# The x loads of experts 0 to 3 as three transfers instead of two, in a batched-expert MLP

## The chip, the cores and the metric

The kernel runs on one core of one Trainium2 chip. The metric is the time of one execution on the device in microseconds (us). Lower is better. The core's engines are named as in the profile: PE (TensorE: matmuls and transposes; PEld is its weight load), DVE (VectorE), ACT (ScalarE), POOL (GpSimd) and SP (SyncE, which here only waits and issues transfers). Transfers run on 16 DMA engines that all issuing engines share.

## What is computed

Eight experts, each with its own input and its own two weight matrices:

```python
n_experts, capacity, hidden, expert_hidden = 8, 256, 512, 2048
# x (8, 256, 512), w1 (8, 512, 2048), w2 (8, 2048, 512), all float32
h = np.matmul(x, w1)
h = np.maximum(h, 0)
return np.matmul(h, w2).astype(np.float32)
```

In float32, one expert's w1 is 4.19 MB, its w2 the same, its x 0.52 MB. The kernel computes in bfloat16 and stores float32.

## The kernel before, in words

Sizes: E = 8 experts, C = 256 rows, H = 512, F = 2048; P = 128 partitions, MT = C / P = 2 row tiles, KT1 = H / P = 4, KT2 = F / P = 16, G = E / 2 = 4.

**Loading x.** x of experts 0 to 3 goes into `x_f` as float32, by transfers that SP issues in `load_x` (line 92). The view `x_r` puts two neighbouring rows of x on one partition, so for each expert a partition gets one piece of 2 x 512 x 4 B = 4 KB; a transfer of one expert is 128 such pieces, of two experts 256. x of experts 4 to 7 goes into `x_c`, cast to bfloat16 on the way, in one transfer that POOL issues (line 139).

**The frame.** Only the x loads of line 92 stand inside the Tile frame. `tc.close()` (line 97) ends it; in the trace the barrier that goes with it is booked under line 98: every engine waits there for every other. All else is issued behind it, with semaphores set by hand.

**POOL's queue behind the barrier.** POOL issues, in this order: x_c (line 139), w1 of experts 0 and 1 (line 129, `load_w1`), builds the identity matrix (lines 142 to 144), w2 of experts 0 and 1 (line 134, `load_w2`). All weights are cast to bfloat16 on the way. There are two buffers for w1 and two for w2, so each further w1 waits until ACT has done the first layer of the expert that holds the buffer, each further w2 until that expert's output is copied. The w2 of the last two experts comes in two parts (lines 136 and 137). The last transfer on POOL's queue is the output of experts 0 to 3 (line 163). SP issues the outputs of experts 4 to 6 (line 123) and 7 (line 125).

**Transposing x.** Four rounds, r = 0 to 3, take two experts each: a = 2r + b, where DVE does b = 0 and ACT does b = 1 (`take_x`). In a round, DVE and ACT each wait for x, cast or copy it into `x_b[:, b]` (line 174, in `cast`) and raise `t_xb`. PE waits until `t_xb` has both (`take(t_xb, 2)`, line 247 on; line 87 is the wait), transposes 8 tiles for each b into `pt[b]` (line 251), and DVE and ACT copy the result to `xe` (line 190 for experts 0 to 3, line 193 for 4 to 7). In rounds 0 and 1 the wait is for `s_x[r]`, the transfer that holds both experts of the round; from round 2 on for x_c.

**The two layers.** PE runs all four rounds of transposes first, then for each pair of experts the first layer of both (line 267, out of `pt_h`, with ReLU by DVE at line 216 and ACT at line 214) and the second layer of both (line 287, into `pt_o`, copied out at line 223). Ahead of each expert's layer PE waits on `t_w`, which SP raises when the weights have landed and, for the first layer, when x is transposed (SP's chain of waits, lines 105 to 125).

Of the kernel before, what the change touches and what calls it, by code (L numbers as in the profile page):

```python
# [9 lines left out]
def kernel(  # L10
# [20 lines left out]
    G = E // 2  # L31
# [28 lines left out]
    pt = [nc.alloc_psum_tensor(f"pt_tr{b}", [P, KT1 * MT, P], bf) for b in range(2)]  # L60

    sem = nc.alloc_semaphore
    s_x = [sem(f"s_x{i}") for i in range(G // 2)]
    s_xc = sem("s_xc")
    s_out = [sem(f"s_out{i}") for i in range(3)]
    s_w1 = [sem(f"s_w1_{e}") for e in range(E)]
# [24 lines left out]
    def load_x(e, n, i):  # L91
        ins = sp.dma_start(x_f[:, e:e + n], x_r[:, e:e + n]).then_inc(s_x[i], 16)
        return ins.ins.name

    for r in range(G // 2):
        tc.no_tile_sem_insts.add(load_x(2 * r, 2, r))
    tc.close()
    tc.compile()  # L98

# [69 lines left out]
    def cast(eng, r, b):  # L169

        a = 2 * r + b
        src = x_f[:, a] if a < G else x_c[:, MT * (a - G):MT * (a - G + 1)]
        copy = act.copy if eng is act else dve.tensor_copy
        copy(  # L174
            x_b[:, b].rearrange("p (t m) q -> p t m q", m=MT),
            src.rearrange("p m (q t) -> p t m q", t=KT1),
        ).then_inc(t_xb, 1)

    def take_x(eng, b):
        copy = act.copy if eng is act else dve.tensor_copy  # L180
        for r in range(G):
            if r < G // 2:
                eng.wait_ge(s_x[r], 16)
            elif r == G // 2:
                eng.wait_ge(s_xc, 16)
            cast(eng, r, b)
            eng.wait_ge(s_tr, 2 * r + b + 1)
            a, n = 2 * r + b, KT1 * C
            if a < G:
                copy(xe[:, a * n:(a + 1) * n], pt[b][:].rearrange("p j q -> p (j q)")).then_inc(s_xe[b], 1)  # L190
            else:
                xl = xe[:, G * n:].rearrange("p (l j q f) -> p l j q f", l=G, j=KT1 * MT, f=G)
                copy(  # L193
                    xl[:, :, :, :, a - G].rearrange("p l j q -> p j l q"),
                    pt[b][:].rearrange("p j (l q) -> p j l q", l=G),
                ).then_inc(s_xe[b], 1)
# [28 lines left out]

    act.sem_inc(t_ha, 1)
    take_x(act, 1)
    layers(act, 1, s_ha, s_oa, t_ha, s_act)

    dve.sem_inc(t_hb, 1)  # L230
    take_x(dve, 0)
    layers(dve, 0, s_hb, s_ob, t_hb, s_dve)

# [95 lines left out]
```

## Time and profile before

| what | value |
|---|---|
| time, median of 3 runs | 179.58 us (179.54 to 179.58) |
| the profiled execution | 179.67 us |
| its span, first to last instruction | 178.4 us |
| mean granted TensorE clock | 0.963 |
| transfers issued in all | 24, of which 2 load `x_f` |

The profile is that of one execution. "us to landing" of a transfer counts from its issue to the last of its 16 completions. Times within the trace are us from the span's start. A transfer's issue is an instruction of the issuing engine's queue (SPq, POOL) and lasts well under a microsecond; the bytes move later, on the DMA engines. GB/s are those written to the destination: a transfer that casts float32 to bfloat16 reads twice what it writes.

### The profile page before, as it was taken

What the parts mean: (1) busy time and instruction counts of PE and PEld (TensorE: products, weight loads), DVE (VectorE), ACT (ScalarE), POOL (GpSimd) and SP (SyncE); (2) the same over time, 40 slices, a digit from 0 to 9 for tenths busy, and PEclk for the clock granted to TensorE, in tenths of its full rate; (3) what the DMA queues carried; (4) which work ended last, traced back from release to release, by engine and by line L of the source; (5) the groups of instructions that cost most, each with busy time, mean ns of one, the idle gap of its engine ahead of it and who ended that gap; (6) DMA issues with size and microseconds to landing.
All of it is one profiled execution on the core that took longest, in us unless ns stands there. A gap on an engine that the chain in (4) does not pass through costs nothing. (4 is left out here: it accounts for less than half of the span.)

```text
span 178.4 us, 2360 instructions
## 1 busy us (share of the span) xinstructions
PE 131.5 (74%) x832; PEld 89.3 (50%) x832; DVE 37.3 (21%) x48; ACT 37.9 (21%) x49; POOL 12.4 (7%) x26
## 2 busy tenths in 40 slices
PE   0214479899949696899769695979495695998950
PEld 0213368796413295794224485954142694953410
DVE  0232653332010133131100231320101141311010
ACT  2455554222010122121100132220101122311010
POOL 3500000101010101001000101010202100000000
PEclk9999999999987999699969999999999999999996
DMA  5999989989989989989999998998998999999998
GB/s 181 349 234 235 228 184 235 235 176 235 235 176 235 235 184 228 235 191 220 235 206 206 235 220 191 235 232 180 235 235 176 235 235 192 201 214 225 280 417 353
DMA packets 4352, 40.90 MB, mean 229 GB/s; under 512 B 384, under 2 KB 384, under 8 KB 2176
## 3 DMA queue, kind: packets, MB, share of 16 engines
q0 software_dynamic: 3264, 36.70, 94.2%
q1 hardware_dynamic: 1088, 4.19, 6.1%
HBM read 71.30 MB, written 4.19 MB: 423 GB/s over the span
## 5 line engine op out<-in xcount | busy, mean ns | idle before, releaser
L267 PE MATMUL pt_h<-xe,w_sb 128*128 x512 | 65.0, 284 | 12.9 <-PEq L87 12.9
L267 PEld LDWEIGHTS pt_h<-xe,w_sb 128*128 x512 | 57.5, 147 | 21.0 <-issue 19.2
L287 PE MATMUL pt_o<-w_sb,ht_sb 128*128 x256 | 59.7, 393 | 9.7 <-PEq L87 9.7
L287 PEld LDWEIGHTS pt_o<-w_sb,ht_sb 128*128 x256 | 25.3, 100 | 42.7 <-issue 16.2
L216 DVE TENSOR_SCALAR ht_sb<-pt_h 128x512 bf16<-128x512 f32 x32 | 22.1, 692 | 51.7 <-PE pt_h L267 51.6
L214 ACT ACTIVATE ht_sb<-pt_h 128x512 bf16<-128x512 f32 x32 | 19.1, 597 | 56.7 <-PE pt_h L267 56.7
L251 PE MATMUL pt_tr<-identity,x_b 128*128 128x128 bf16 x64 | 7.5, 309 | 17.7 <-PEq L87 17.7
L223 DVE COPY out_sb<-pt_o 128x512 f32 x8 | 5.5, 692 | 66.1 <-PE pt_o L287 66.1
L223 ACT COPY out_sb<-pt_o 128x512 f32 x8 | 4.7, 586 | 64.3 <-PE pt_o L287 64.3
L251 PEld LDWEIGHTS pt_tr<-identity,x_b 128*128 128x128 bf16 x64 | 6.5, 143 | 18.4 <-issue 18.4
L129 POOL DMA_DIRECT2D w_sb<-in_w_dram x8 | 4.3, 534 | 71.3 <-ACTq L218 71.3
L134 POOL DMA_DIRECT2D w_sb<-in_w_dram x6 | 3.9, 652 | 35.3 <-ACT out_sb L223 35.2
L193 DVE COPY xe<-pt_tr 128x1024 bf16<-128x1024 bf16 x2 | 4.9, 2466 | 5.2 <-PE pt_tr L251 5.2
L193 ACT COPY xe<-pt_tr 128x1024 bf16<-128x1024 bf16 x2 | 4.9, 2465 | 4.1 <-PE pt_tr L251 4.1
L174 ACT CAST x_b<-x_f 128x1024 bf16<-128x1024 f32 x2 | 4.0, 2000 | 2.9 <-DMA x_f<-in_x_dram 2.9
L174 DVE CAST x_b<-x_f 128x1024 bf16<-128x1024 f32 x2 | 2.2, 1076 | 7.9 <-DMA x_f<-in_x_dram 7.9
L190 ACT COPY xe<-pt_tr 128x1024 bf16<-128x1024 bf16 x2 | 2.0, 1012 | 4.1 <-PE pt_tr L251 4.1
L190 DVE COPY xe<-pt_tr 128x1024 bf16<-128x1024 bf16 x2 | 1.4, 692 | 4.2 <-PE pt_tr L251 4.2
L136 POOL DMA_DIRECT2D w_sb<-in_w_dram x2 | 1.1, 531 | 17.0 <-ACT out_sb L223 17.0
L174 ACT COPY x_b<-x_c 128x1024 bf16<-128x1024 bf16 x2 | 2.2, 1118 | 0.0
L174 ACT ACT_TABLE_LOAD x1 | 1.3, 1283 | 2.6 <-PEq L98 2.6
L174 DVE COPY x_b<-x_c 128x1024 bf16<-128x1024 bf16 x2 | 1.4, 700 | 0.0
(9 smaller groups left out, 3.4 us busy)
## 6 DMA issues: line engine op xcount, KB each, us to landing
w_sb<-in_w_dram POOLq DMA_DIRECT2D x14, 2048.0 KB, 29.5
w_sb<-in_w_dram POOLq DMA_DIRECT2D x2, 1152.0 KB, 26.7
x_f<-in_x_dram SPq DMA_DIRECT2D x2, 1024.0 KB, 7.7
out_dram<-out_sb POOLq DMA_DIRECT2D x1, 2048.0 KB, 36.0
w_sb<-in_w_dram POOLq DMA_DIRECT2D x2, 896.0 KB, 30.4
out_dram<-out_sb SPq DMA_DIRECT2D x1, 1536.0 KB, 8.6
x_c<-in_x_dram POOLq DMA_DIRECT2D x1, 1024.0 KB, 9.9
out_dram<-out_sb SPq DMA_DIRECT2D x1, 512.0 KB, 5.8
```

What stands on the lines that cost most here:

```text
L129: pool.dma_start(w1_k[:, e % 2 * KT1:(e % 2 + 1) * KT1], w1_r[e]).then_inc(s_w1[e], 16)
L134: pool.dma_start(w2_k[:, k:k + KT2], w2_r[e]).then_inc(s_w2[e], 16)
L136: pool.dma_start(w2_k[:, k:k + CUT], w2_r[e, :, :CUT]).then_inc(s_w2[e], 16)
L174: copy(x_b[:, b].rearrange("p (t m) q -> p t m q", m=MT), src.rearrange("p m (q t) -> p t m q", t=KT1),).then_inc(t_xb, 1)
L190: copy(xe[:, a * n:(a + 1) * n], pt[b][:].rearrange("p j q -> p (j q)")).then_inc(s_xe[b], 1)
L193: copy(xl[:, :, :, :, a - G].rearrange("p l j q -> p j l q"), pt[b][:].rearrange("p j (l q) -> p j l q", l=G),).then_inc(s_xe[b], 1)
L214: act.activation(dst, ph[half][:], relu).then_inc(t_h, 1)
L216: dve.tensor_relu(dst, ph[half][:]).then_inc(t_h, 1)
L223: copy(outs[b], po[:, half]).then_inc(s_copied, 1)
L251: ins = pe.transpose(pt[b][:, j], x_b[:, b, j], identity[:])
L267: ins = pe.matmul(ph[i // 2][:, i % 2, :], ws[i % 2 * KT1 + kt], xs[kt], start=(kt == 0), stop=(kt == KT1 - 1),)
L287: ins = pe.matmul(po[:, m], hs[(kt - k0) * MT + m], ws[kt - k0], start=(kt == 0), stop=(kt == KT2 - 1),)
```

## The change

x of experts 0 and 1 comes in one transfer each (128 pieces of 4 KB), x of experts 2 and 3 together in a third (256 pieces). All three are issued by SP inside the frame, ahead of the barrier. There are three semaphores. In round 0 DVE waits for the first transfer and ACT for the second; in round 1 both wait for the third.

```diff
-    s_x = [sem(f"s_x{i}") for i in range(G // 2)]
+    s_x = [sem(f"s_x{i}") for i in range(3)]
...
-    for r in range(G // 2):
-        tc.no_tile_sem_insts.add(load_x(2 * r, 2, r))
+    for i, (e, n) in enumerate(((0, 1), (1, 1), (2, 2))):
+        tc.no_tile_sem_insts.add(load_x(e, n, i))
     tc.close()
     tc.compile()
...
         for r in range(G):
             if r < G // 2:
-                eng.wait_ge(s_x[r], 16)
+                eng.wait_ge(s_x[b if r == 0 else 2], 16)
             elif r == G // 2:
                 eng.wait_ge(s_xc, 16)
             cast(eng, r, b)
```

## The prediction

> **What bounds the kernel now.** I read the DMA parts of the page first, because the program moves far more bytes than it computes.
>
> ```profile
> q0 software_dynamic: 3264, 36.70, 94.2%
> HBM read 71.30 MB, written 4.19 MB: 423 GB/s over the span
> PE pt_o L287 4%; ACT out_sb L223 0%
> PE 131.5 (74%) x832; PEld 89.3 (50%) x832; DVE 37.3 (21%) x48; ACT 37.9 (21%) x49; POOL 12.4 (7%) x26
> ```
>
> POOL's queue alone holds the 16 DMA engines for 94.2% of the span; no compute engine is above 74%. (The third row is the chain of waits by line, 4% of the span.) The next view cuts the span into stretches; the last two columns are the mean busy share of the DMA engines (packets overlap a little, so a full one reads just over 1) and the GB/s moved.
>
> ```profile
> 0.00:1.50 1.50, 0.00 (x0) 0.00 (x0) 0.00 (x0) 0.00 (x0) 0.20 (x4) 1.00 0.00 0
> 1.50:2.50 1.00, 0.00 (x0) 0.00 (x0) 0.00 (x0) 0.00 (x0) 0.00 (x0) 1.00 0.81 61
> 2.50:3.00 0.50, 0.00 (x0) 0.00 (x0) 0.00 (x0) 0.45 (x1) 0.01 (x1) 1.00 0.61 246
> 3.00:6.50 3.50, 0.00 (x0) 0.00 (x0) 0.87 (x1) 1.71 (x2) 3.13 (x6) 1.00 1.03 424
> 6.50:7.50 1.00, 0.00 (x0) 0.00 (x0) 0.22 (x1) 1.00 (x1) 0.87 (x2) 1.00 1.08 332
> 7.50:9.00 1.50, 1.22 (x12) 1.25 (x13) 0.17 (x1) 0.14 (x1) 0.00 (x0) 1.00 1.06 251
> 9.00:11.00 2.00, 0.65 (x7) 0.38 (x4) 0.52 (x1) 1.01 (x1) 0.00 (x0) 1.00 1.09 254
> 11.00:13.00 2.00, 0.00 (x0) 0.00 (x0) 1.07 (x1) 1.22 (x1) 0.00 (x0) 1.00 1.25 262
> 13.00:168.30 155.30, 126.13 (x801) 86.26 (x802) 33.72 (x44) 31.80 (x45) 8.18 (x15) 0.97 1.01 216
> 168.30:174.30 6.00, 3.54 (x17) 1.40 (x15) 0.69 (x1) 0.59 (x1) 0.00 (x0) 1.00 1.03 423
> 174.30:177.50 3.20, 0.00 (x0) 0.00 (x0) 0.00 (x0) 0.00 (x0) 0.00 (x0) 0.68 1.03 422
> 177.50:178.40 0.90, 0.00 (x0) 0.00 (x0) 0.00 (x0) 0.00 (x0) 0.00 (x0) 0.50 0.12 46
> ```
>
> From 3.0 to 177.5 us no stretch falls below 1.01: the DMA engines have no hole, even in the tail, where the chain of waits names PE and ACT. (Weights show 216 GB/s and not 424 because float32 is read and half the bytes, bfloat16, are written.) So the end is the moment when bytes begin to flow, about 2.5 us, plus a fixed amount of packet work, plus holes, of which there are none. The change can move the time by moving that start, by adding packet work, or by opening a hole. The order of transfers within the busy stretch doesn't matter to the sum.
>
> What starts the queues, in order of time (start us, duration us):
>
> ```profile
> 0.74 0.95 SPq L92 DMA_DIRECT2D x_f<-in_x_dram  x2
> 2.55 1.28 ACT L174 ACT_TABLE_LOAD   x1 [2.55 <-PEq L98]
> 2.99 0.68 POOL L139 DMA_DIRECT2D x_c<-in_x_dram  x1 [2.54 <-POOLq L98]
> 3.66 1.07 POOL L129 DMA_DIRECT2D w_sb<-in_w_dram  x2
> 5.18 0.28 POOL L144 TENSOR_SCALAR_AFFINE_SELECT identity<-identity 128x128 bf16<-128x128 bf16 x1 [0.24 <-POOL identity L142]
> 5.63 2.01 ACT L174 CAST x_b<-x_f 128x1024 bf16<-128x1024 f32 x1 [1.79 <-DMA x_f<-in_x_dram]
> 7.78 1.86 PE L251 MATMUL pt_tr<-identity,x_b 128*128 128x128 bf16 x16 [7.78 <-PEq L87]
> 9.68 1.01 ACT L190 COPY xe<-pt_tr 128x1024 bf16<-128x1024 bf16 x1 [2.04 <-PE pt_tr L251]
> 11.78 1.99 ACT L174 CAST x_b<-x_f 128x1024 bf16<-128x1024 f32 x1 [1.08 <-DMA x_f<-in_x_dram]
> 24.98 9.35 PE L267 MATMUL pt_h<-xe,w_sb 128*128 x64
> 51.85 8.75 PE L287 MATMUL pt_o<-w_sb,ht_sb 128*128 x32 [2.35 <-PEq L87]
> ```
>
> The frame's end is a barrier at L98. Its rows by source line (min/median/max ns, first to last start):
>
> ```profile
> L98 SPq DRAIN  x3: 7/7/128, 1.7 to 2.2; - x3
> L98 ACTq DRAIN  x2: 8/8/8, 0.8 to 2.2; - x2
> ```
>
> ACT stands at the barrier at 0.8 us, SP only at 1.7, after its two x issues. SP is the last to come, so whatever SP issues inside the frame delays every engine, and POOL's weight queue first of all.
>
> **The change, part by part.** The rows by source line for SP's issues, here and at the end of the program, the landings in us (the row without a name is that of the first w1 issue alone), and the page's small packets:
>
> ```profile
> L92 SPq DMA_DIRECT2D x_f<-in_x_dram x2: 433/446/459, 0.7 to 1.2; - x2
> L125 SPq DMA_DIRECT2D out_dram<-out_sb x1: 356/356/356, 172.5 to 172.5; - x1
> x_f<-in_x_dram SPq DMA_DIRECT2D x2, 1024.0 KB, 7.7
> x_c<-in_x_dram POOLq DMA_DIRECT2D x1, 1024.0 KB, 9.9
> DMA to landing us min/median/max: 19.0/19.0/19.0
> DMA packets 4352, 40.90 MB, mean 229 GB/s; under 512 B 384, under 2 KB 384, under 8 KB 2176
> ```
>
> (1) *One more issue ahead of the barrier.* Two issues took 0.95 us: 0.433 + 0.459 and one gap of 0.06. No load of 128 rows is in the trace; the nearest row is the store of 128 rows at L125, 0.356. Three issues take at least 2 x 0.356 + 0.433 + 0.11 = 1.26 us, at most 3 x 0.459 + 0.11 = 1.49. So all engines leave the frame 0.31 to 0.54 us later; I take 0.42. POOL's x_c issue goes from 2.99 to 3.4, both w1 from 3.66 to 4.1, the identity from 5.46 to 5.9, ACT's table load from 2.55 to 3.0.
>
> None of this is on the path, and x_f's own bytes are the cover. They are 2 x 1024 KB = 2.10 MB; the first three stretches move 0.06 + 0.12 = 0.18 MB by 3.0 us, and the remaining 1.91 MB take 4.5 us at 424 GB/s. Undisturbed they keep the engines busy until 7.5. x_c's packets now begin inside 6.5 to 7.5: that stretch averages 332, halfway between 424 and the 251 behind it, so the switch falls near 7.0. A shift of 0.42 puts it at 7.4, still ahead of 7.5. If the time between x_c's issue and its first packet (4 us now) is partly waiting behind x_f's packets, the margin is larger. If the cover went, the whole stream would come later by what is left of the delay. The first w1 needs no cover: it lands at 3.66 + 19.0 = 22.7, behind x_c at 2.99 + 9.9 = 12.9, so it stands in the queue for microseconds anyway. Identity and table load are needed at 7.78 and 5.6. Term: 0, bounds 0 to +0.54.
>
> (2) *A smaller first transfer.* Bytes flow 1.8 us after the first issue starts. If that lag counts from the issue's end, a first issue of 0.356 instead of 0.433 brings 0.08; if from its start, nothing; if issuing went in proportion to rows, 0.22. I take 0.04 (between the first two, nearest L125). Term: -0.04, bounds -0.22 to 0. The 512 KB of expert 0 take 1.2 us to move, and the second issue follows within 0.5, so no hole opens between them.
>
> (3) *Sixteen more completion packets.* 24 transfers have 384 packets under 512 B: 16 each, one per engine. The first x transfer's sixteen fall inside the stretch 3.00:6.50 (ACT's cast, which waits for it, starts at 5.63), which shows no dip below 1.03. Term: +0.01, bounds 0 to 0.05.
>
> (4) *Waits.* No wait is added; three are retargeted. DVE (b = 0) now waits for expert 0 alone, ACT for expert 1, both for the third transfer in round 1. Expert 0 lands 1.2 us sooner, at about 4.4, and DVE casts then. But PE takes both casts together, and ACT's cast of expert 1, whose bytes are as far back as before, still starts near 5.6 and takes 2.01. PE's first transposes stay at 7.8: this gain is not used.
>
> (5) *x of experts 2 and 3.* Their last packets share the engines with x_c from 7.0 on and land just ahead of ACT's second cast at 11.78; with x_c 0.4 later they get further alone. ACT is free at 9.68 + 1.01 = 10.69, so its second cast can start at 10.7 instead of 11.78, and all behind it comes up to 1.1 us earlier, PE's first layer-1 matmul at 23.9 instead of 24.98 (w1 has landed at 22.7). That gain ends at 51.85, where PE already waits 2.35 us for weights. Term: 0.
>
> Sum: 0 - 0.04 + 0.01 = -0.03. The profiled execution took 179.67 us (span 178.4, 1.3 outside it), giving 179.64; the median of the runs is 0.09 below the profiled one, so **179.55 us**.
>
> "DMA: Bandwidth & Descriptors" of the Trainium skill (Anatomy of one DMA; Bandwidth) speaks against the change: each DMA has a fixed cost of about 2 us and should carry at least 1 MiB, so one transfer more would give an estimate of 181.6. By the trace that cost doesn't repeat while another transfer is queued, as rival C below works out from rows.
>
> **The rivals.**
>
> *B, a hole between x_f and x_c (slower).* Place: the 16 engines at 7.5 us. If x_c's lag behind its issue is fixed, its packets come 0.31 to 0.54 later; the mean margin is 0.5, but the engines need not switch together, and one that switches only at 7.5 loses up to 0.54, keeps it to the end, and the end waits for the last engine: **180.1**. It decides from a delay above the margin, and grows if the third issue blocks SP until an earlier transfer lands. Against it: the third issue brings no more rows than before (512 in all), and the present second took only 0.03 longer than the first. Chance 0.09.
>
> *C, each transfer pays its start again (slower).* From issue to bytes is 0.74 to 2.5, 1.8 us; paid once more, 179.6 + 1.8 = **181.4**. Against it: 3.00:6.50 spans the end of the first transfer and the start of the second at 424 GB/s. Chance 0.03.
>
> *D, the first bytes come sooner by the whole 0.22* of term 2: **179.35**; with the engines drifting apart less, up to half of this case goes below 179.22. For it: nothing but the missing row. Chance 0.06.
>
> *E, PE's 1.1 us carries to the end:* **178.5**. That the change doesn't reach the first transposes is already in the forecast; this needs layer 1, not the weights, to set the pace, against the 2.35 us wait at 51.85. Chance 0.04.
>
> **How the numbers follow.** The forecast has 0.78. This measurement can tell about 0.2%, 0.36 us: 179.22 to 179.94. Slower: B and C, 0.12. Faster: E and half of D, 0.07. Same: 0.78 + 0.03 = 0.81. The range goes from term 2's lower bound with some drift of the engines, 179.25, to most of B, 180.0; C, E, half of D and the top of B stay outside, under 0.2.
>
> **What would show it.** Three x_f issues from 0.74, ending near 2.1; x_c issued at 3.3 to 3.5; DVE's first cast near 4.4 and ACT's still near 5.6; first transposes at 7.8; ACT's second cast near 10.7; the first w1 still landing at 22.7 and DMA share above 1 from 3.0 to 177.5. I am wrong if the stretch around 7.5 us falls below 1 (B), if bytes flow visibly sooner than 2.5 (D), if the 512 KB transfers leave a dip before 6.5 (C), or if the wait at 51.85 is gone (E).

## The result, and the profile after

The changed kernel takes 180.72 us (median of 11 runs, 179.77 to 181.45) against 179.62 us before (179.46 to 179.96): a ratio of 1.0054, 95% interval 1.0041 to 1.0066. It is 1.1 us slower, outside the range of the prediction, and its own runs scatter over 1.7 us where those of the kernel before scatter over 0.5: two of the eleven, 179.77 and 179.87, lie among those of the kernel before. The profiled execution took 180.60 us with a span of 179.3.

The stretches of the changed kernel, as for the kernel before (last two columns: share of the DMA engines, GB/s):

```profile
1.50:2.50 1.00, 0.00 (x0) 0.00 (x0) 0.00 (x0) 0.00 (x0) 0.00 (x0) 1.00 0.69 168
2.50:3.00 0.50, 0.00 (x0) 0.00 (x0) 0.00 (x0) 0.04 (x1) 0.00 (x0) 1.00 1.04 418
3.00:6.50 3.50, 0.00 (x0) 0.00 (x0) 1.07 (x1) 2.44 (x2) 2.87 (x5) 1.00 0.92 352
6.50:7.50 1.00, 0.08 (x2) 0.11 (x3) 0.00 (x0) 0.78 (x1) 0.87 (x3) 1.00 1.24 381
...
13.00:168.30 155.30, 126.04 (x784) 86.69 (x790) 33.78 (x44) 30.99 (x44) 8.14 (x15) 0.96 1.01 216
...
177.50:178.40 0.90, 0.00 (x0) 0.00 (x0) 0.00 (x0) 0.00 (x0) 0.00 (x0) 0.50 0.41 164
178.40:179.30 0.90, 0.00 (x0) 0.00 (x0) 0.00 (x0) 0.00 (x0) 0.00 (x0) 0.50 0.08 32
```

Three things are to be seen. First, the bytes flow sooner: 168 KB + 209 KB = 377 KB by 3.0 us (a packet's bytes count at its start), where the kernel before had 184; the 193 KB more are 0.46 us at 424 GB/s. Second, the stretch from 3.0 to 6.5 is no longer full: 0.92 and 352 GB/s in place of 1.03 and 424. Third, the end frays out: in the last 0.9 us the share is 0.08, about one engine of 16, where the kernel before had 0.12 in its last 0.9 with all engines stopping close together. A finer cut of the same view finds the hole behind 4.5 us, where the third x transfer begins (by then 377 + 618 = 995 KB of the 1,049 KB of the first two have moved):

```profile
3.00:4.50 1.50, 0.00 (x0) 0.00 (x0) 0.42 (x1) 1.24 (x1) 1.11 (x2) 1.00 1.01 412
4.50:5.50 1.00, 0.00 (x0) 0.00 (x0) 0.64 (x1) 0.21 (x1) 1.00 (x2) 1.00 0.80 299
5.50:6.50 1.00, 0.00 (x0) 0.00 (x0) 0.00 (x0) 1.00 (x1) 0.76 (x3) 1.00 0.89 315
```

The same cut of the kernel before:

```profile
3.00:4.50 1.50, 0.00 (x0) 0.00 (x0) 0.00 (x0) 0.83 (x1) 1.50 (x3) 1.00 1.03 423
4.50:5.50 1.00, 0.00 (x0) 0.00 (x0) 0.00 (x0) 0.00 (x0) 0.73 (x3) 1.00 1.02 418
5.50:6.50 1.00, 0.00 (x0) 0.00 (x0) 0.87 (x1) 0.87 (x1) 0.91 (x1) 1.00 1.04 430
```

The timeline and the rows by source line of the changed kernel at its start:

```profile
0.74 1.35 SPq L92 DMA_DIRECT2D x_f<-in_x_dram  x3
3.39 0.67 POOL L139 DMA_DIRECT2D x_c<-in_x_dram  x1 [2.94 <-POOLq L98]
4.06 1.73 POOL L129 DMA_DIRECT2D w_sb<-in_w_dram  x2
4.08 1.07 DVE L174 CAST x_b<-x_f 128x1024 bf16<-128x1024 f32 x1 [4.08 <-DMA x_f<-in_x_dram]
5.29 1.99 ACT L174 CAST x_b<-x_f 128x1024 bf16<-128x1024 f32 x1 [1.06 <-DMA x_f<-in_x_dram]
7.42 1.87 PE L251 MATMUL pt_tr<-identity,x_b 128*128 128x128 bf16 x16 [7.42 <-PEq L87]
10.24 1.99 ACT L174 CAST x_b<-x_f 128x1024 bf16<-128x1024 f32 x1
24.59 2.76 PE L267 MATMUL pt_h<-xe,w_sb 128*128 x12 [0.96 <-PEq L87]
```

```profile
L98 SPq DRAIN  x3: 7/7/123, 2.1 to 2.6; - x3
L92 SPq DMA_DIRECT2D x_f<-in_x_dram x3: 393/422/427, 0.7 to 1.7; - x3
```

SP reaches the barrier at 2.1 instead of 1.7, and POOL issues x_c at 3.39 instead of 2.99. PE's first layer waits 0.96 us for the first w1, which it did not do before.

A transfer raises its semaphore 16 times; with 16 DMA engines, each of these completions is taken here as that of one engine. The completions, read out of the trace for the first w1 and for the last transfer of the program, tell how far the engines have drifted apart (us; the eighth-last of 16 stands for the middle):

```
                 first w1: first  middle  last     last output: first  middle  last
kernel before             22.34   22.52  22.63                 177.86  178.02  178.31
changed kernel            22.46   22.81  23.82                 177.91  178.17  179.24
```

The fastest engine is 0.12 us later than before, the middle one 0.29, the slowest 1.19. Most of a lag from the first microseconds is still there at the end: the last output ends 0.93 us later. The second x transfer completes within 0.33 us (4.94 to 5.27), x_c within 1.32 (12.78 to 14.10, in the kernel before 12.66 to 12.91), so the engines part between the two.

The packets of the trace show how. From 3.0 to 6.5 us the kernel before has 16 packets open at any time, one for each engine. In the changed kernel this falls to between 10 and 12 from 4.75 to 5.5 us: about five engines have nothing to do while the others go on. In the mean, the holes are 234 KB, 0.55 us at 424 GB/s, little more than the 0.46 us that the early start brought. Most of the 1.1 us is that the engines don't share them evenly. Where the loss begins is therefore clear from the profile alone: in holes in x_f's own packets between 4.5 and 6.5 us, unequal among the engines. Why they are there is not.

### The profile page after: what moved, and what is told of

The parts are those of the page before. It is cut to its first block, busy times and chain, and to the rows that moved or that the text cites. A ratio compares the mean times of both kernels' runs of the same rounds, so it can differ in the third digit from the quotient of the medians.

```text
span 179.3 us, 2353 instructions
## 1 busy us (share of the span) xinstructions
PE 133.2 (74%) x824; PEld 90.9 (51%) x832; DVE 37.3 (21%) x48; ACT 37.7 (21%) x49; POOL 12.3 (7%) x26
## 5 line engine op out<-in xcount | busy, mean ns | idle before, releaser
L267 PE MATMUL pt_h<-xe,w_sb 128*128 x512 | 68.3, 294 | 13.9 <-PEq L87 13.9
L267 PEld LDWEIGHTS pt_h<-xe,w_sb 128*128 x512 | 59.5, 148 | 23.5 <-issue 20.2
L287 PE MATMUL pt_o<-w_sb,ht_sb 128*128 x248 | 57.8, 387 | 9.7 <-PEq L87 9.3
## 6 DMA issues: line engine op xcount, KB each, us to landing
x_c<-in_x_dram POOLq DMA_DIRECT2D x1, 1024.0 KB, 10.7
```

Source lines behind the costliest of these rows:

```text
L267: ins = pe.matmul(ph[i // 2][:, i % 2, :], ws[i % 2 * KT1 + kt], xs[kt], start=(kt == 0), stop=(kt == KT1 - 1),)
L287: ins = pe.matmul(po[:, m], hs[(kt - k0) * MT + m], ws[kt - k0], start=(kt == 0), stop=(kt == KT2 - 1),)
```

## The experiments

Three theories stood at the start. **Theory 1:** DVE's early cast. POOL's first w1 issue now takes as long as DVE's cast beside it. **Theory 2:** the later barrier, that is rival B of the prediction. **Theory 3:** a third x transfer as such. Others were formed on the way; the expectations number them on. Each run is compared with the kernel before on the same chip; the chips differ between the groups e1 to e4, e5 to e9, f and g, and h is on that of e1.

**e1_dve_waits_both.**

```diff
-                eng.wait_ge(s_x[b if r == 0 else 2], 16)
+                if r == 0:
+                    eng.wait_ge(s_x[0], 16)
+                eng.wait_ge(s_x[1 if r == 0 else 2], 16)
```

> The changed kernel with one edit: in round 0 DVE and ACT both wait for the first two transfers, so DVE's first cast moves from 4.08 to about 5.3 us and lies beside ACT's; the three transfers and the later barrier stay. Theory 1 (DVE's early cast keeps POOL from issuing w1 of expert 0, 1.21 us instead of 0.54, and that leaves holes between 4.5 and 6.5): holes gone, first bytes 0.4 us sooner than before the change, about 179.2. Theory 2 (the barrier, 0.4 us later, opens a hole between x_f and x_c): unchanged, 180.7. Theory 3 (the third x transfer starts up slowly, whatever else goes on): holes stay at 4.6 to 6.5, 180.7.

Measured 181.01 us, ratio 1.0071 (1.0059 to 1.0084). DVE's cast went to 5.41 us and the first w1 issue was back at its usual length (two in 1.07 us). The loss stayed. Its stretches:

```profile
4.50:5.50 1.00, 0.00 (x0) 0.00 (x0) 0.09 (x1) 0.12 (x1) 0.85 (x3) 1.00 0.99 348
5.50:6.50 1.00, 0.00 (x0) 0.00 (x0) 0.98 (x1) 1.00 (x1) 0.91 (x1) 1.00 0.96 369
```

On the mean the holes are smaller than in the changed kernel, yet the first w1 completes from 22.36 to 23.97, the last but one engine at 23.12: one engine carries most of the loss. Added up from 1.5 to 6.5 us, e1 has moved as much as the kernel before (1.67 MB each). So the mean rate can't show this loss; 15 packets instead of 16 are open from 4.75 to 5.75 us. Theory 1 falls.

**e2_two_transfers_1_3**, transfers `((0, 1), (1, 3))`, the wait `s_x[b if r == 0 else 1]`.

> Two x transfers, as before the change, but of expert 0 alone and of experts 1 to 3; DVE casts expert 0 early, ACT waits for the second transfer, which now ends late, so round 0 is late too. The barrier stands where it stood before the change. Theory 1 (DVE's early cast against POOL's issues): a POOL issue near 4.1 us still stretched to about 1.2, holes stay, 180 to 181. Theory 2 (later barrier): holes gone, 179.2 to 179.6. Theory 3 (a third transfer): no third transfer, holes gone, 179.2.

Measured 179.80 us, 1.0006 (0.9998 to 1.0015): no loss to speak of, though DVE's early cast (4.18 us) stretched a POOL issue here too. The first bytes came as early as in the change (143 and 360 GB/s up to 3.0 us), and still there is no gain: first w1 from 22.24 to 22.81.

**e3_big_first**, transfers `((0, 2), (2, 1), (3, 1))`, the wait `s_x[0 if r == 0 else 1 + b]`.

> Three x transfers, but experts 0 and 1 in the first and 2 and 3 in one each: DVE's first cast is back at about 5.6 us, the barrier is as late as in the change. Theory 1 (early cast): no holes, 179.6 like the kernel before. Theory 2 (later barrier): 180 to 180.7. Theory 3 (start-up of the later transfers of one expert): a hole near 5 or 6.3, 180 to 181.

Measured 179.74 us, 1.0005 (0.9996 to 1.0013). Three transfers, x_c issued at 3.47 us, later than in the change, and no hole:

```profile
3.47 0.67 POOL L139 DMA_DIRECT2D x_c<-in_x_dram  x1 [3.02 <-POOLq L98]
4.50:5.50 1.00, 0.00 (x0) 0.00 (x0) 0.00 (x0) 0.00 (x0) 0.92 (x3) 1.00 1.04 426
5.50:6.50 1.00, 0.00 (x0) 0.00 (x0) 0.83 (x1) 0.83 (x1) 0.71 (x2) 1.00 1.02 418
```

Theories 2 and 3, as put, fall together.

**e4_pool_late**, in the kernel before: the memset of the identity ahead of the x_c issue.

> The kernel before with one edit: the memset of the identity stands ahead of the x_c issue on POOL, so x_c and the weights are issued 0.3 to 0.4 us later with two x transfers and no early cast. Theory 2 (a later POOL queue opens a hole between x_f and x_c): 180.0 or more. Theories 1 and 3: 179.6, no hole, since x_f's packets last until 7.5.

Inconclusive: the memset hid in the time that POOL needs ahead of a transfer anyway, and x_c was issued at 3.02 instead of 2.99. 179.67 us, 1.0001 (0.9992 to 1.0009). What it was to show, e3 shows.

**e5_late_short** and **e6_late_long.** Only experts 0 and 1 in the frame, the rest behind `tc.compile()`, in two transfers and in one:

```diff
-    for i, (e, n) in enumerate(((0, 1), (1, 1), (2, 2))):
-        tc.no_tile_sem_insts.add(load_x(e, n, i))
+    for i in range(2):
+        tc.no_tile_sem_insts.add(load_x(i, 1, i))
     tc.close()
     tc.compile()
+    for i in range(2, 4):       # e5; e6: load_x(2, 2, 2)
+        load_x(i, 1, i)
```

> Experts 0 and 1 in one transfer each inside the frame, experts 2 and 3 in one transfer of 128 rows each, issued by SP behind the barrier; four semaphores. POOL's x_c issue is back at about 2.95 us. Theory 4 (a transfer of 256 rows takes longer to set up than one of 128, and as the third it comes too late for its first packets): all transfers short, no hole between 4.5 and 6.5, and the first bytes still 0.4 to 0.5 us sooner than in the kernel before, so 179.2. Theory 2 (later barrier): no late barrier, 179.2 too. Theory 3 (any third transfer that follows two short ones): holes, 180.7.

> As e5_late_short, but experts 2 and 3 come together in one transfer of 256 rows behind the barrier. Theory 4 (the 256-row transfer is set up late): issued some 0.8 us later than in the change, so holes as large as there or larger, 181 or more. Theory 2 (the barrier alone): 179.2. Theory 3: 180.7.

Measured 179.89 us, 1.0013 (1.0002 to 1.0024), runs from 179.50 to 180.65; and 180.02 us, 1.0023 (1.0011 to 1.0035), runs from 179.51 to 180.82. Neither theory has this: the long one, issued later than in the change, loses less, and the short ones still lose in some executions. e5's profiled execution is one of those (180.44): it moves 242 and 340 GB/s in the two microseconds from 4.5, but with shares of 1.08 and 0.96, so its packets take long rather than that engines stand idle. Theory 4 falls in its first form.

**e7_four_short**, transfers `((0, 1), (1, 1), (2, 1), (3, 1))` in the frame, four semaphores, the wait `s_x[2 * r + b]`.

> Four transfers of 128 rows, all inside the frame, so the barrier and POOL's issues come another 0.4 us later than in the change. Theory 4: no hole between 4.5 and 6.5; x_f would be through near 7.0, x_c's first packets come 3.7 to 3.9 us behind an issue at about 3.8, at 7.6, so a hole of some 0.5 us between them that eats the sooner start: 179.6 to 179.9. Theory 2 (barrier): worse than the change, 181 or more. Theory 3: 180.7 or more.

Measured 180.91 us, 1.0067 (1.0054 to 1.008). The forecast of theory 4 is missed. Part of the loss may have a cause of its own, seen in the timeline:

```profile
3.85 1.50 POOL L139 DMA_DIRECT2D x_c<-in_x_dram  x1 [3.41 <-POOLq L98]
4.16 1.06 DVE L174 CAST x_b<-x_f 128x1024 bf16<-128x1024 f32 x1 [4.16 <-DMA x_f<-in_x_dram]
```

Here it is x_c's issue that runs beside DVE's cast and takes 1.50 us instead of 0.67; h2 below takes that away.

**e9_quiet_pool**, the change with eight chained memsets ahead of POOL's x_c issue, which moves to 6.10 us.

> The changed kernel with eight memsets of the identity chained ahead of POOL's x_c issue, so POOL issues no transfer until about 7 us. The time is not the point: with a fixed lag of 3.8 us from x_c's issue to its packets it rises by about 4 us. If POOL's issues or its descriptors are what starves x_f, the stretches from 4.5 to 6.5 are full (share 1.02). Theory 4 (the third transfer by itself): they stay below 1 as in the change.

One run, 183.09 us, most of it by the late x_c. POOL issued nothing before 6.1, and the hole is the largest of all:

```profile
4.50:5.50 1.00, 0.00 (x0) 0.00 (x0) 0.63 (x1) 0.10 (x1) 0.94 (x2) 1.00 1.17 217
5.50:6.50 1.00, 0.00 (x0) 0.00 (x0) 0.00 (x0) 1.00 (x1) 0.64 (x3) 1.00 0.60 246
```

(The share of 1.17 beside 217 GB/s comes of packets that took up to 1.3 us, where 0.16 is usual.) So POOL's queue is not what starves x_f. x_c's lag isn't fixed either: its first packet begins at 7.50, 1.4 us behind the issue, where the kernel before needs 3.9 (2.99 to 6.84).

**f1_one_transfer**, `load_x(0, 4, 0)` alone, and **f2_half_bytes**, four short transfers with `x_f[:, e:e + n, 0]` and `x_r[:, e:e + n, 0]`; DVE sets the other half of `x_f` to zero ahead of the casts.

> x of all four experts in one transfer of 512 rows; every wait of rounds 0 and 1 is for it; one issue in the frame, so the barrier comes some 0.5 us earlier than in the kernel before. Theory 5 (SP's transfers are set up one after the other at about the pace at which the bytes move, 128 rows in some 1.1 us, and a transfer's first bytes wait for a part of its set-up that grows with its rows): first bytes not at 2.65 but at 3.5 to 4, then no hole, and the end later by as much, 180.4 to 181. Theory 4 (only a third transfer is slow): first bytes at 2.65, 179.6.

> Four transfers of 128 rows of 2 KB instead of 4 KB: every second row of x of experts 0 to 3 is left out and DVE writes zeros in its place, so the kernel moves 1 MB less and computes with half of that x. It measures the set-up by itself: by the bytes the four would be through 0.62 us apart. Theory 5: they land 1.0 to 1.2 us apart all the same, with the share between 3 and 6 near 0.6. Theory 4, and any by which only reads or writes of the bytes are slow: 0.6 to 0.7 us apart, share near 1 until they are through.

f1: 179.98 us, 1.0019 (1.001 to 1.0028); 66 GB/s from 1.5 to 2.5, 221 from 2.5 to 3.0, that is a start like that of 256 rows and not at 3.5 to 4. It is 0.35 us slower than the kernel before, with a dip of its own (369 GB/s from 3.0 to 4.5) that no theory had. f2, one run: the last completions of the four lie at 3.36, 4.68, 5.34 and 6.03 us, the first ones at 2.80, 3.58, 4.23 and 5.04, so 0.65 to 0.81 apart from first to first and 1.32, 0.66 and 0.69 from last to last. Apart from the one 1.32, a set-up of 1.0 to 1.2 us for 128 rows isn't there. Theory 5 falls.

**f3_third_on_act**, **f4_one_each** and, later, **g4_second_on_act** let ACT issue a part at the head of the frame (`load_x` gets the issuing engine as an argument):

```diff
+    for e, n, i, q in ((0, 1, 0, sp), (2, 2, 2, act), (1, 1, 1, sp)):   # f3
+    for e, n, i, q in ((0, 1, 0, sp), (1, 3, 1, act)):                  # f4
+    for e, n, i, q in ((0, 1, 0, sp), (1, 1, 1, act), (2, 2, 2, sp)):   # g4
+        tc.no_tile_sem_insts.add(load_x(e, n, i, q))
```

> The three transfers of the change, but the third, experts 2 and 3, is issued by ACT at the head of the frame, beside SP's two, so it is issued at 0.8 instead of 1.66 us and in a queue of its own; the barrier is back where it was before the change. Theory 5 with one set-up for both queues: the third no longer late, but it shares the engines with the first two from the start; first bytes at 2.1 to 2.7, holes small, 179.2 to 180. Theory 5 with a set-up for each queue: no holes, 179.2. If the holes belong to the length of the first transfer alone, they stay, 180.7.

> Two transfers, expert 0 from SP and experts 1 to 3 from ACT, both at the head of the frame, so the barrier comes about 0.45 us earlier than in the kernel before. Theory 5 with a set-up for each queue: first bytes near 2.1 from SP, ACT's follow at 2.5 to 3.5 while SP's last, 179.2 to 179.6. Theory 5 with one set-up for both: a hole near 3.3 once expert 0 is through, 180 or more.

f3: 179.51 us, 0.9994 (0.9985 to 1.0002): the loss is gone, and the engines are together again (first w1 22.30 to 22.62).

```profile
3.00:4.50 1.50, 0.00 (x0) 0.00 (x0) 0.00 (x0) 0.75 (x1) 1.50 (x3) 1.00 1.00 341
4.50:5.50 1.00, 0.00 (x0) 0.00 (x0) 0.53 (x1) 0.00 (x0) 0.76 (x3) 1.00 1.01 410
```

It gives its early start back between 3.0 and 4.5 (341 GB/s), once. f4: 179.65 us, 0.9999 (0.999 to 1.0008). Taking the third out of SP's queue removes the loss. But f3 also issues it 0.9 us sooner and brings the barrier back, so the queue alone isn't shown to be the reason; and no version with the loss was run on this chip.

Still open was which feature of the queue it is: a short first transfer (theory 6), the long one as the third (theory 7), or the number in one queue (theory 8).

**g1_short_long_short**, transfers `((0, 1), (1, 2), (3, 1))`, the wait `s_x[(b, 1 + b)[r]]`.

> Three transfers from SP in the frame: expert 0, experts 1 and 2, expert 3 (128, 256, 128 rows). Theory 6 (a short first transfer starts the bytes 0.45 us sooner without a reserve, and whatever stands behind it in the same queue comes in with holes): bytes early, holes, engines spread, 180.3 to 181. Theory 7 (the loss belongs to the 256-row transfer as the third): 179.2 to 179.7.

Measured 179.61 us, 0.9994 (0.9986 to 1.0003). This is the sharpest control: the same three issues as the change, the same rows in all, the same late barrier (x_c at 3.42), the same early first bytes; the second and third differ in length, and with them the waits: ACT's first cast now waits for 256 rows.

```profile
1.50:2.50 1.00, 0.00 (x0) 0.00 (x0) 0.00 (x0) 0.00 (x0) 0.00 (x0) 1.00 0.70 205
2.50:3.00 0.50, 0.00 (x0) 0.00 (x0) 0.00 (x0) 0.02 (x1) 0.00 (x0) 1.00 1.02 393
4.50:5.50 1.00, 0.00 (x0) 0.00 (x0) 0.55 (x1) 0.00 (x0) 1.00 (x2) 1.00 0.97 389
5.50:6.50 1.00, 0.00 (x0) 0.00 (x0) 0.00 (x0) 0.00 (x0) 0.69 (x3) 1.00 1.05 422
```

A small dip is left at 4.5 (0.97, 389), and the engines end together (first w1 22.01 to 22.64). Theories 6 and 8, as put, fall.

**g2_late_long_on_act**: e6 with `load_x(2, 2, 2, act)`. **g3_row_first**: the change with a transfer of `x_r[:, 0:2, 0, :P]` into a spare tensor ahead of the three.

> As e6_late_long (experts 0 and 1 in the frame, experts 2 and 3 together behind the barrier), with the late transfer issued by ACT instead of SP. Theory 8 (three one behind the other in one queue are what hurts): no holes behind 4.5, 179.2 to 179.4. Theory 6 (early start without a reserve, in any queue): as e6, 179.8 to 180.2.

> The change with one more transfer ahead of the three, of 256 rows of 512 B into a buffer that nobody reads (131 KB, some 0.3 us of packets), so SP issues four in the frame and the barrier comes 0.4 us later still. Theory 6: the early start is gone, no holes between 4.5 and 6.5, about 179.9 (before plus 0.3). Theory 8 (number of transfers in the queue): holes as in the change or larger, 181 or more.

> The three transfers of the change with the second, expert 1, issued by ACT at the head of the frame; SP issues expert 0 and experts 2 and 3. No queue holds more than two, the barrier is back at its old place. Theory 8: no loss, 179.2 to 179.6 as f3_third_on_act. Theory 6: a short first in both queues and 256 rows behind it, holes near 4, 180 or more.

g2: 179.87 us, 1.002 (1.0005 to 1.0035), with seven runs from 179.50 to 179.92 and four from 180.17 to 180.77, so a loss of about 1 us that comes and goes, though the third was in ACT's queue; with e5 and e6 this stays unexplained. g3: 181.21 us, 1.0088 (1.0069 to 1.0107): taking the early start away doesn't help, and of the 1.5 us lost only 0.3 are its own packets. Here the third of the three is reached near 5.5 us, and there the hole is (332 GB/s from 5.5 to 6.5, 14 packets open instead of 16 from 5.75 to 6.0); 341 GB/s from 3.0 to 4.5 are a second loss, with all engines busy. g4: 179.64 us, 0.9994 (0.9985 to 1.0003), with the first bytes late (66 GB/s from 1.5 to 2.5).

What separates the runs with the whole loss (the change, e1, e7, g3, and e9 by its hole) from those without (e2, e3, g1, f3, f4, g4) is now one feature: **a transfer that stands in SP's queue right behind two short ones.** It is not the only difference. In the change the third is needed near 4.6 us, in e3 and g1 only near 6, when three quarters of x_f have moved; no run keeps two short ones ahead and moves the third's turn that far back, so a third that is merely needed too soon remains a rival. Nor is the feature all: e5 and e6 have it too and lose in some executions only, and g2 loses without it. Theory 9 gave it a mechanism with a size.

**h2_four_short_dve_late**: e7 with the waits of e1 in round 0. **h1_short_long_late**: g1 with `load_x(3, 1, 2)` behind `tc.compile()`.

> e7_four_short with DVE's first cast beside ACT's (round 0 waits for both transfers), so that it no longer stretches POOL's x_c issue; against e1_dve_waits_both only the third transfer is split in two. Theory 9 (an engine takes on a queue's third transfer only when the first is through there, and its first bytes then need as long as from the issue at the start: 1.3 us for 128 rows, 1.9 for 256): the third is taken on near 3.4 and ready at 4.7, the second lasts until 4.6, so the hole is near 0.1 instead of 0.6, and 179.3 to 180.0, the rest from the barrier, 0.4 us later still. If two short transfers at the head hurt whatever follows: 180.7 to 181.

> g1_short_long_short (expert 0; experts 1 and 2; expert 3) with the third transfer issued behind the barrier, so POOL's x_c issue is back near 2.95 us. Theory 9: the third is needed at 5.8 and ready by then, first bytes near 2.1, no hole: 179.2 to 179.5, below the kernel before. If a third in SP's queue that comes late always costs: 179.9 as e6_late_long.

h2: 180.49 us, 1.005 (1.0038 to 1.0062), between the two forecasts and nearer to that of two short ones hurting whatever follows.

```profile
4.50:5.50 1.00, 0.00 (x0) 0.00 (x0) 0.21 (x1) 0.24 (x1) 1.00 (x3) 1.00 0.88 291
5.50:6.50 1.00, 0.00 (x0) 0.00 (x0) 0.86 (x1) 1.00 (x1) 0.99 (x2) 1.00 0.96 369
```

The hole begins where theory 9 puts it, at the start of the third, and is over sooner than in the change (369 GB/s against 315 from 5.5 on), but it is several times the 0.1 us that the theory gives a third of 128 rows: (424 - 291) + (424 - 369) = 188 KB, 0.44 us (first w1 22.39 to 23.49). The place of theory 9 fits the runs with the whole loss, its size doesn't fit h2. h1: 179.51 us, 0.9993 (0.9984 to 1.0001), all eleven runs from 179.47 to 179.69: with f3, g1 and g4 (0.9994 each) the best of all versions, but not clear of the kernel before.

## Why the prediction was wrong, by its own steps

**What bounds the kernel.** Right, and it explains the loss: the end is the start of the bytes plus packets plus holes. The sum was kept for the mean of the engines, though; the end goes by the slowest, which went from 22.63 to 23.82 in the first w1, where the middle engine lost 0.29.

**Term 1, the later barrier.** Forecast 0.42 us, measured 0.40 (x_c from 2.99 to 3.39), and its price of 0 is borne out: e3 and g1 issue x_c at 3.47 and 3.42 and lose nothing. The lag of x_c is partly waiting, as the prediction allowed: it is 1.4 us in e9 and in f2 (3.86 to 5.25), against 3.9 in the kernel before.

**Term 2, the smaller first transfer.** This is the step that failed, twice over. Its size: the bytes came 0.46 us sooner, outside the bounds of 0 to 0.22. The lag it reckons with isn't what changed. The first packet begins at 1.82 us before and at 1.77 after; but the first fifteen packets of the kernel before take 0.70 to 0.97 us each, and none has ended by 2.5 us, where the changed kernel's first sixteen take 0.19 to 0.53 and 23 have ended. And its place: it asks for a hole between the first and the second transfer, where there is none (412 GB/s from 3.0 to 4.5), and puts the start of the third at nothing without a word. In its place the runs show the hole at the third (299 and 315 GB/s from 4.5 to 6.5), with the slowest engine 1.19 us late by the first w1 and 0.93 at the end, which is the loss. The third had been issued by 2.1 us, more than 2 us before it was needed: an issue instruction that has ended says nothing of when the transfer can run.

**Term 3, the completion packets.** e3 has the same sixteen more and full stretches; no run sees their price.

**Term 4 and 5, the casts.** DVE's cast at 4.08 (forecast 4.4), ACT's at 5.29 (5.6), transposes at 7.42 (7.8): all 0.3 to 0.4 sooner, by the early start. ACT's second cast at 10.24 (10.7). The first layer came at 24.59, not 23.9, since its weights were late. That none of this reaches the end was right.

**The rivals.** C named the sign that was seen, a dip ahead of 6.5 us, and was given 0.03. Its mechanism is still wrong: three transfers that each paid a start would cost as much in e3 and g1. It was dismissed by one boundary in the trace of before, between two transfers of 256 rows, which shows nothing of short ones. The fixed cost per transfer that the Trainium skill states ("DMA: Bandwidth & Descriptors", Anatomy of one DMA; the section is on transfers that GpSimd issues, and those here are SP's) points to the right side but isn't what happened: by e3 and g1 a third transfer is free, by the change it costs 1.1 us. B had the rule by which one late engine sets the end, at the wrong place: 7.5 us instead of 4.5 to 6.5, so its 180.1 fell short. D was right about the sooner bytes and did not see what eats them. E had no part.

**What stays open.** Shown: the loss begins in x_f's packets, at the start of the transfer behind two short ones in SP's queue, and is uneven among the engines; neither POOL, nor DVE's cast, nor the barrier, nor a third transfer as such makes it. Not shown: why such a transfer starts late and on some engines only; whether it is the two short ones ahead or how soon it is needed; and why e5, e6 and g2 lose about 1 us in some executions only, and the change itself next to nothing in two of eleven.

## What to carry to other kernels

When transfers are what bounds a kernel, reckon with the slowest DMA engine, not with the mean share: compare the first and the last of a transfer's 16 completions early in the program, because most of a lag there stayed to the end here. Splitting the head of a queue into short transfers moved bytes sooner, but two short ones in a row could starve what follows; a long one first or second (e3, g1, h1) or a second issuing queue from the start (f3, g4) avoided it. The gain of an early start was small even then (at best 0.9993, not clear of 1): in g1 the slowest engine has no part in it.

## What the runs showed of the hardware that was not expected

- The first packets of a first transfer of 128 rows begin when those of one of 256 do (1.77 and 1.82 us) but are through about half a microsecond sooner: 168 against 61 GB/s from 1.5 to 2.5 us. From 256 to 512 rows there is no such step (66 GB/s in f1). In g4, where SP and ACT each begin with 128 rows, the sooner bytes are missing too (66 GB/s).
- In g1 the fastest engine completes the first w1 at 22.01, 0.33 us ahead of the kernel before, the slowest at 22.64 against 22.63: an early start is handed to the engines unequally.
- DVE's cast of float32 in SBUF holds up a POOL issue beside it until just after the cast's end: the first of two in 4.06 to 5.79 ran beside a cast that ended at 4.08 + 1.07 = 5.15, and the two took 1.73 us together, against 1.07 when the cast was elsewhere (e1); in e7 x_c's issue ended at 5.35, its cast at 5.22. The Trainium skill describes this for a float32 copy from SBUF to SBUF ("SBUF — State Buffer", SBUF: two separate sides): while DVE runs it, GpSimd can't write the descriptors of its transfers. The traces agree, here for a copy that casts to bfloat16. The kernel before has it too: an issue of w2 beside the cast at 5.63 takes 1.25 us, so an issue doesn't always last well under a microsecond. In the changed kernel it isn't what costs time, since e1 loses as much without it; between e7 and h2, where x_c was hit, the medians differ by 0.4 us, but the two ran on different chips and their intervals overlap.
